# Weight loads of the second pass on GpSimd's DMA queue, pool-branch stores on SyncE's

## The chip, the core and the metric

The kernel runs on one core of a Trainium2 chip. The metric is the device time of one execution in microseconds (us). The engines are TensorE (PE in the rows), VectorE (DVE), ScalarE (ACT), GpSimd (POOL) and SyncE (SP); SP does nothing but issue transfers. Each issuing engine goes through its instructions in order: an instruction that waits for a semaphore holds up everything behind it on that engine, transfers included.

## What is computed

One hybrid encoder layer on x of 1024 x 2048 in float32, from the reference:

```python
h = rmsnorm(x, pre_g) * (1.0 + scale[:, None]) + shift[:, None]   # shift, scale, gate from silu(c) @ w_ada
q, k, v, gate_a, u, gate_p = jnp.split(h @ w_in, SPLIT_POINTS, axis=-1)      # w_in: 2048 x 4608
y_a = windowed_gqa(q, k, v, rel_table, sink) * jax.nn.silu(gate_a)           # 8 heads, window 128
y_p = multiscale_pool(u, w_pool_grp, pool_scale) * jax.nn.silu(gate_p)       # windows 2, 4, 8, 16
g_a, g_p = jnp.split(jax.nn.sigmoid(h @ w_merge + b_merge), 2, axis=-1)      # w_merge: 2048 x 4096
merged = g_a * (y_a @ w_br_attn) + g_p * (y_p @ w_br_pool)                   # branches: 1024 x 2048 each
o = merged @ w_out
return x + gate[:, None] * rmsnorm(o, post_g)
```

The pooling subtracts each token from the mean of a window around it, multiplies per group with a 256 x 256 matrix, and scales.

## The kernel before

Every float32 product is made of three fast ones: each operand is split into a high part (`hi`, ScalarE rounds it) and a low rest (`lo`, VectorE subtracts), and hi x hi, hi x lo and lo x hi are summed in PSUM. On top of that the large products use a scheme of Strassen's kind: 7 block products in place of 8, named B11, T3, T2, B21, T4, T1, B22 after the moving operand (`strassen`, line 183; `product`, line 203). One call of `strassen` is a *pair*: 256 columns of weights against half of the contraction (1024 rows). A product is 12 matmuls of 128 x 512, a pair 84. The results go through three kinds of PSUM banks, X, V and Z.

The projection by `w_in` and `w_merge` has 34 pairs of columns. The contraction is done in two passes: the first writes partial sums to DRAM (`part_d`), the second (`next_pair`, line 885) reads them back (`part<-part_d`, four loads of 256 KB per pair, line 180), adds, and stores the result to `proj_d` (line 282). Beside the second pass' pairs run, as `side` steps, the attention (`step`, line 1000) and then the pooling (`pool_steps`, line 1101). Then come the two branch products, attention and pool, 8 pairs each (line 1165), and the product by `w_out`.

The weights of a pair come as two loads of 512 KB (`load_raws`, line 162; the loads are line 173), one for each half of the contraction rows: tiles `raw` of 128 partitions x 4 pieces x 256 columns, thus 512 pieces of 1 KB. Four buffers hold two pairs. `fetch_weights` (line 287) is called at step 1 of a pair, and loads the weights of a later pair into the buffers of an earlier one as soon as VectorE has read these for the last time. From `raw` VectorE forms sums of blocks (`raw<-raw,raw`, line 104 or 107; `ws<-raw`), and `prep` (line 197) splits them into `whi` and `wlo`, four buffers each.

Before the change all these loads are issued by SP, whose queue also carries the partial sums, the stores of results, the gates `g` and stores `ya_d<-g` of the attention, and the gates `gt` of the branches. GpSimd (`side_load`, `side_store`, line 111) carries in the stretch of the change only the pooling's transfers: `u` (line 1040), the gate `sil` (line 1044, two buffers) and the store of the finished tile `yp_d<-sil` (line 1099); the next `sil` load into a buffer waits until the store from it has landed. `u` has two buffers, set free by VectorE. The order in which instructions stand on each engine is laid down when the program is built, by a scheduler that estimates durations; so a change of a queue can also move rows on VectorE and ScalarE.

Of the kernel before, what the change touches and what calls it, by code (L numbers as in the profile page):

```python
# [20 lines left out]
P = 128  # L21
# [21 lines left out]
def encoder_layer(ctx: ExitStack, tc: tile.TileContext, x, c, table, w_ada, b_ada, pre_g,  # L43
# [21 lines left out]
    def pool(name, bufs=1, **kw):  # L65
        return tc.tile_pool(name=name, bufs=bufs, reuse_waits="tile", **kw)
# [10 lines left out]
    def uid(s):  # L77
        cnt[0] += 1
        return f"{s}_{cnt[0]}"

    def bank(tag, name="b"):
        return psum.tile([P, 512], F32, tag=tag, name=uid(name), bufs=1 if tag in SEEDED else 2)
# [8 lines left out]
    def split(hi, lo, src):  # L91
        last_hi[0] = nc.scalar.activation(hi, src, AF.Copy)  # L92
        last_split[0] = nc.vector.tensor_tensor(lo, src, f32(hi), ALU.subtract)  # L93
        return last_split[0]
# [8 lines left out]
    def add(o, a, b, eng=None):  # L103
        (eng or nc.vector).tensor_tensor(o, a, b, ALU.add)  # L104
# [2 lines left out]
        (eng or nc.vector).tensor_tensor(o, a, b, ALU.subtract)  # L107

    load = nc.sync.dma_start
    store = nc.sync.dma_start  # L110
    side_load = side_store = nc.gpsimd.dma_start

# [21 lines left out]
    yp_d = dram.tile([NH * P, S], F32, name="yp_d")  # L134
# [23 lines left out]
    def ktile(kh, j):  # L158

        return 2 * j + kh  # L160

    def load_raws(w, n0, row0, js):

        nj = len(js)
        r0 = row0 + ktile(0, js[0]) * P
        rows = w[r0:r0 + 2 * nj * P, n0:n0 + 256].rearrange("(j k p) n -> k p j n", k=2, p=P)
        if nj == 2:
            r = wp.tile([P, 2, 2, 256], F32, tag="raw", name=uid("raw"), bufs=4)
            halves = [r[:, 0], r[:, 1]]
        else:  # L170
            halves = [wp.tile([P, 4, 256], F32, tag="raw", name=uid("raw"), bufs=4) for _ in range(2)]
        for kh in range(2):
            load(halves[kh], rows[kh])
        return [[h[:, :, nt * P:(nt + 1) * P] for h in halves] for nt in range(2)]

    def load_parts(ev, part):
# [110 lines left out]
    def fetch_weights():  # L287
        if wanted_w:
            fetched.append(load_raws(*wanted_w.popleft(), range(4)))
# [40 lines left out]
    rows = ev.tile([P, 512], F32, tag="ev", name="rows")[0:104, 0:P]  # L330
# [187 lines left out]
    def all_of(steps):  # L518
        for s_ in steps:
            s_()  # L520

    fetch_rows_of_x(0)
    fetch_rows_of_x(1)
    raws = [load_raws(*weight_of(ORDER[0]), 0, (0, 1))]
    ada = [ada_slots(0, load)]
    first_w = [slot("wf") for _ in range(3)]
# [39 lines left out]
    ada.append(ada_slots(1, load))  # L566
    claim((1,))
    raws += [load_raws(*weight_of(ORDER[i]), 0, (0, 1)) for i in (1, 2)]
    mark = const.tile([P, 1], F32, name="mark")
    come = ada[1][KT - 3][:, 0, 0:1]  # L570
# [120 lines left out]
    i = RAMP  # L691
# [111 lines left out]
    halves = deque()  # L803
# [75 lines left out]
    assert not side  # L879
    all_of(before)  # L880
    op = op2
    pidx = [0]
    side = deque()

    def next_pair(every=(0, 1, 3, 4, 6), then=None):
        n = ORDER[pidx[0]]
        w, n0 = weight_of(n)
        run(strassen(w, n0, HALF * P, range(4), op, to_dram(block(proj_d, n)),
                     block(part_d, n)), side, every, None, then)
        pidx[0] += 1  # L890
# [140 lines left out]
    with pool("pool") as pp:  # L1031
        pooled, sil = {}, {}

        us, sg, wg = {}, {}, {}

        def fetch_u(i):
            us[i] = pp.tile([P, S + 2 * PAD], F32, tag="u", name=f"u{i}", bufs=2)
            nc.gpsimd.memset(us[i][:, 0:PAD], 0.0)
            nc.gpsimd.memset(us[i][:, S + PAD:S + 2 * PAD], 0.0)
            side_load(us[i][:, PAD:PAD + S], proj_d[COL_U + i * P:COL_U + (i + 1) * P, :])  # L1040

        def fetch_sg(i):
            sg[i] = pp.tile([P, S], F32, tag="sil", name=f"sil{i}", bufs=2)
            side_load(sg[i], proj_d[COL_GP + i * P:COL_GP + (i + 1) * P, :])

        def fetch_wg(g):
            wg[g] = pp.tile([P, 2, 256], F32, tag="wg", name=f"wg{g}")
            load(wg[g], w_pg[g].rearrange("(k p) n -> p k n", p=P))

        def split_wg(g):  # L1050
            gh = pp.tile([P, 2, 256], F32R, tag="wgh", name=f"wgh{g}")
            gl = pp.tile([P, 2, 256], F32R, tag="wgl", name=f"wgl{g}")
            split(gh, gl, wg[g])
            wg[g] = gh, gl

        def window(i, w):

            cur, n = us[i], 1
            lo_, hi_ = 0, S + 2 * PAD
            while n < w:  # L1060
                if n == 4:
                    yield
                nxt = pp.tile([P, S + 2 * PAD], F32, tag="win", name=f"win{i}_{n}", bufs=2)
                d0, d1 = (1, 0) if n == 1 else (n // 2, n // 2)
                lo_, hi_ = lo_ + d0, hi_ - d1
                add(nxt[:, lo_:hi_], cur[:, lo_ - d0:hi_ - d0], cur[:, lo_ + d1:hi_ + d1])
                cur, n = nxt, 2 * n
            if w <= 4:
                yield
            win = cur[:, PAD:PAD + S]  # L1070
            for e in list(range(w // 2)) + list(range(S - w // 2 + 1, S)):
                n_e = min(S, e + w // 2) - max(0, e - w // 2)
                nc.vector.tensor_scalar(win[:, e:e + 1], win[:, e:e + 1], float(w) / n_e, None,
                                        op0=ALU.mult)
            yield
            nc.vector.scalar_tensor_tensor(win, win, 1.0 / w, us.pop(i)[:, PAD:PAD + S],
                                           op0=ALU.mult, op1=ALU.subtract)
            hi = pp.tile([P, S], F32R, tag="phi", name=f"phi{i}", bufs=2)
            lo = pp.tile([P, S], F32R, tag="plo", name=f"plo{i}", bufs=2)
            split(hi, lo, win)  # L1080
            pooled[i] = (hi, lo)
            yield

        def mix(g, j):
            i = 2 * g + j
            gh, gl = wg[g]
            t = sg.pop(i)
            wn = slice(j * P, (j + 1) * P)
            for s in range(2):
                sl = slice(s * 512, (s + 1) * 512)  # L1090
                ps = bank("at")
                for k in range(2):
                    hi, lo = pooled[2 * g + k]
                    nc.tensor.matmul(ps, gh[:, k, wn], hi[:, sl], start=k == 0, stop=False)
                    nc.tensor.matmul(ps, gh[:, k, wn], lo[:, sl], start=False, stop=False)
                    nc.tensor.matmul(ps, gl[:, k, wn], hi[:, sl], start=False, stop=k == 1)
                nc.vector.scalar_tensor_tensor(t[:, sl], ps, cols[:, 96 + i:97 + i], t[:, sl],
                                               op0=ALU.mult, op1=ALU.mult)
            side_store(yp_d[i * P:(i + 1) * P, :], t)

        def pool_steps(g, w):
            i = 2 * g
            first, second = window(i, w), window(i + 1, w)

            def silu(i):
                nc.scalar.activation(sg[i], sg[i], AF.Silu)

            return [lambda: (next(first), fetch_wg(g), fetch_u(i + 1)),
                    lambda: next(first),
                    lambda: (next(first), fetch_sg(i)),  # L1110
                    lambda: (next(second), split_wg(g)),
                    lambda: (next(second), fetch_sg(i + 1)),
                    lambda: (next(second), fetch_u(i + 2) if g < 3 else None),
                    lambda: (silu(i), silu(i + 1), mix(g, 0)),
                    lambda: mix(g, 1)]

        for g, w in enumerate(POOLS):
            side.extend(pool_steps(g, w))
        fetch_u(0)
        while side:  # L1120
            next_pair((1, 2, 4, 5))
        while side:
            next_pair((2, 5))
# [41 lines left out]
    for b, w in enumerate((w_ba, w_bp)):  # L1165
# [4 lines left out]
        else:  # L1170
# [6 lines left out]
            for _ in range(2):  # L1177
                t = mr.tile([P, 2, 512], F32, tag="raw2", name=uid("mt"), bufs=2)
# [424 lines left out]
```

## Time and profile before

| | us |
|---|---|
| median of 3 runs (lowest to highest) | 2133.7 (2130.52 to 2135.07) |
| the profiled execution | 2130.04 |
| its span, first to last instruction | 2128.0 |
| TensorE busy in the span | 2078.3 (98%) |
| VectorE busy | 1502.8 (71%) |
| ScalarE busy | 1082.4 (51%) |
| GpSimd busy | 195.6 (9%) |
| transfers of SP's queue (q1) | 345.58 MB |
| transfers of GpSimd's queue (q0) | 100.85 MB |

A share of busy time is an average over the whole span; what a stage can lose or gain is read from that stage's rows. The granted clock of TensorE is 1.00 of full speed in practically all of the span. The stages by time: the first pass to about 740 us, four plain pairs of the second pass to about 808, attention to about 1170, pooling to about 1362, plain pairs to about 1500, the branches to about 1830, then the product by `w_out`.

### The profile page before, as it was taken

To read this page: it belongs to the slowest core of one execution; us is meant where nothing else is said; L and a number is where in the kernel's file an instruction comes from. 1 tells how busy PE (TensorE), PEld (TensorE's weight loads), DVE (VectorE), ACT (ScalarE), POOL (GpSimd) and SP (SyncE) were. 2 spreads that over 40 slices of the span, in tenths; PEclk is the share of its full clock that TensorE was granted. 3 is DMA by queue.
4 is the path that set the end of the run, shared out by engine and by line. 5 is a ranking of instruction groups with operands and counts; after the bars stand their busy time and mean duration, and the time that the engine had idled before them with its cause. 6 is when DMAs were issued, how large, how long until landed. Compare 5 with 4: busy or idle time off the path is not lost.

```text
span 2128.0 us, 29020 instructions
## 1 busy us (share of the span) xinstructions
PE 2078.3 (98%) x9628; PEld 1709.8 (80%) x9628; DVE 1502.8 (71%) x2701; ACT 1082.4 (51%) x2005; POOL 195.6 (9%) x424
## 2 busy tenths in 40 slices
PE   5999999999999999999999999999999999999997
PEld 3688788888888888888888878788788887788886
DVE  6788577775456867777686678757857977655568
ACT  6664434443554635777676334234645645545343
POOL 1402132221022100000000000000000000000012
PEclk9999999999999999999999999999999999999999
DMA  9778688885566555555445666565665646877258
GB/s 343 279 232 308 227 279 294 285 294 172 170 214 226 191 183 188 165 165 193 159 163 158 213 217 216 190 214 174 202 208 167 205 139 203 271 245 235 96 177 306
DMA packets 268334, 455.62 MB, mean 214 GB/s; under 512 B 23538, under 2 KB 119930, under 8 KB 268184
## 3 DMA queue, kind: packets, MB, share of 16 engines
q1 hardware_dynamic: 234016, 345.58, 49.8%
q0 software_dynamic: 30256, 100.85, 14.1%
q10 hardware_dynamic: 3912, 7.34, 1.1%
q8 instruction: 76, 1.25, 0.2%
q14 instruction: 74, 0.61, 0.1%
HBM read 321.53 MB, written 134.24 MB: 214 GB/s over the span
## 4 chain that ended last, share of the span: by engine, by line
PE 85%; DMA 7%; DVE 5%; issue 2%; ACT 1%; SPq 0%; DVEq 0%; POOL 0%; ACTq 0%; POOLq 0%
PE Z L207 29%; PE V L207 20%; PE X L207 19%; PE OUT L1292 11%; DMA ada<-in_w_ada_dram 1%; DVE wlo L93 1%; DMA xt<-in_x_dram 1%; PE PT L980 1%; DVE po L1504 1%; DMA sil<-proj_d 1%; DMA m_d<-pv 1%; DMA proj_d<-p 1%; DMA lm<-m_d 1%; DMA pv<-mp_d 0%; PE SCORE L958 0%
## 5 line engine op out<-in xcount | busy, mean ns | idle before, releaser
L92 ACT ACTIVATE whi<-raw 128x512 fp32r<-128x512 f32 (+1 forms) x537 | 320.4, 601 | 456.5 <-PE Z L207 245.8
L93 DVE TENSOR_TENSOR wlo<-raw,whi 128x512 fp32r<-128x512 f32 (+1 forms) x537 | 347.8, 652 | 140.2 <-PE Z L207 78.1
L92 ACT ACTIVATE whi<-wr 128x512 fp32r<-128x512 f32 x112 | 69.6, 627 | 103.3 <-PE OUT L1292 95.4
L93 DVE TENSOR_TENSOR wlo<-wr,whi 128x512 fp32r<-128x512 f32 x112 | 75.8, 687 | 64.5 <-ACT whi L92 64.5
L104 DVE TENSOR_TENSOR u<-V,u 128x512 f32<-128x512 f32 x90 | 62.0, 689 | 73.5 <-PE V L207 70.0
L92 ACT ACTIVATE whi<-ws 128x512 fp32r<-128x512 f32 (+1 forms) x90 | 54.1, 601 | 109.2 <-PE V L207 107.8
L104 DVE TENSOR_TENSOR raw<-raw,raw 128x512 f32<-128x512 f32 x78 | 53.8, 689 | 59.3 <-DMA raw<-in_w_merge_dram 37.7
L207 PE MATMUL Z<-B22h,whi 128*128 128x512 f32 x334 | 92.0, 393 | 3.7 <-ACT u L256 2.4
L207 PE MATMUL V<-T3h,whi 128*128 128x512 f32 x334 | 91.6, 393 | 1.8 <-ACT whi L92 1.8
L207 PE MATMUL Z<-T1h,whi 128*128 128x512 f32 x334 | 91.0, 390 | 2.0 <-ACT u L218 1.5
L207 PE MATMUL X<-B11h,whi 128*128 128x512 f32 x334 | 91.7, 392 | 0.0
L207 PE MATMUL V<-T4h,whi 128*128 128x512 f32 x334 | 91.3, 392 | 0.0
L207 PE MATMUL Z<-T2h,whi 128*128 128x512 f32 x334 | 90.7, 391 | 0.4 <-ACT Z L233 0.4
L207 PE MATMUL X<-B21h,whi 128*128 128x512 f32 x334 | 90.8, 391 | 0.0
L207 PE MATMUL V<-T4l,whi 128*128 128x512 f32 x334 | 90.7, 390 | 0.0
L207 PE MATMUL Z<-B22l,whi 128*128 128x512 f32 x334 | 90.5, 390 | 0.0
L207 PE MATMUL V<-T3h,wlo 128*128 128x512 f32 x334 | 90.5, 390 | 0.0
L207 PE MATMUL V<-T3l,whi 128*128 128x512 f32 x334 | 90.5, 390 | 0.0
L207 PE MATMUL X<-B11l,whi 128*128 128x512 f32 x334 | 90.5, 390 | 0.0
L207 PE MATMUL X<-B21l,whi 128*128 128x512 f32 x334 | 90.4, 390 | 0.0
L207 PE MATMUL X<-B11h,wlo 128*128 128x512 f32 x334 | 90.4, 390 | 0.0
L207 PE MATMUL Z<-T1l,whi 128*128 128x512 f32 x334 | 90.4, 389 | 0.0
(418 smaller groups left out, 5108.9 us busy)
## 6 DMA issues: line engine op xcount, KB each, us to landing
part<-part_d SPq DMA_DIRECT2D x136, 256.0 KB, 4.1
raw<-in_w_merge_dram SPq DMA_DIRECT2D x64, 512.0 KB, 5.4
raw<-in_w_in_dram SPq DMA_DIRECT2D x60, 512.0 KB, 4.8
ada<-in_w_ada_dram POOLq DMA_DIRECT2D x96, 256.0 KB, 6.4
proj_d<-part SPq DMA_DIRECT2D x68, 256.0 KB, 2.2
gada<-in_w_ada_dram POOLq DMA_DIRECT2D x32, 512.0 KB, 5.8
gt<-proj_d SPq DMA_DIRECT2D x64, 256.0 KB, 3.2
wr<-ws_d SPq DMA_DIRECT2D x32, 512.0 KB, 4.9
```

The lines of the kernel that those rows point to most:

```text
L92: last_hi[0] = nc.scalar.activation(hi, src, AF.Copy)
L93: last_split[0] = nc.vector.tensor_tensor(lo, src, f32(hi), ALU.subtract)
L104: (eng or nc.vector).tensor_tensor(o, a, b, ALU.add)
L207: last_mm[0] = nc.tensor.matmul(ps, w_[:, i], op[mov][j][m_], start=fresh and i == 0 and n == 0, stop=i == nj - 1 and n == 2, skip_group_c ...
L980: nc.tensor.transpose(pt[:, i * P:(i + 1) * P], p[:, i * P:(i + 1) * P], ident)
L1292: nc.tensor.matmul(banks[t], m_[:, ts_], w_, start=fresh and j == 0 and n == 0, stop=j == KS - 1 and n == 2, skip_group_check=True)
L1504: last_lo[0] = nc.vector.scalar_tensor_tensor(o_, o_, s_[:, 2:3], rows_x[si][n], op0=ALU.mult, op1=ALU.add)
```

## The change

`load_raws` issues its loads through a cell, `raw_load[0]`. The cell holds SP's queue at first and is set to GpSimd's where the second pass begins, and stays so for the branches. The store of the pooling's finished tile goes from GpSimd's queue to SP's.

```diff
     load = nc.sync.dma_start
+    raw_load = [load]
     store = nc.sync.dma_start
     side_load = side_store = nc.gpsimd.dma_start
...
         for kh in range(2):
-            load(halves[kh], rows[kh])
+            raw_load[0](halves[kh], rows[kh])
...
     all_of(before)
     op = op2
+    raw_load[0] = side_load
     pidx = [0]
...
                 nc.vector.scalar_tensor_tensor(t[:, sl], ps, cols[:, 96 + i:97 + i], t[:, sl],
                                                op0=ALU.mult, op1=ALU.mult)
-            side_store(yp_d[i * P:(i + 1) * P, :], t)
+            store(yp_d[i * P:(i + 1) * P, :], t)
```

TensorE's order is the same before and after. GpSimd's order at the end of attention, where the pooling's first loads stand; before:

```order
L772 DMA ws_d_102<-xt_6564 128x512
L1038 MEMSET u_11549 128x8
L1039 MEMSET u_11549 128x8
L1040 DMA u_11549<-proj_d 128x1024
L1038 MEMSET u_11613 128x8
L1039 MEMSET u_11613 128x8
L1040 DMA u_11613<-proj_d 128x1024
L1044 DMA sil_11677<-proj_d 128x1024
L1044 DMA sil_11780<-proj_d 128x1024
```

The same place after the change (`raw_11585` and `raw_11586` are the two halves of one pair's weights):

```order
L174 DMA raw_11419<-in_w_merge_dram 128x4x256
L174 DMA raw_11585<-in_w_merge_dram 128x4x256
L1040 MEMSET u_11549 128x8
L1041 MEMSET u_11549 128x8
L1042 DMA u_11549<-proj_d 128x1024
L1040 MEMSET u_11613 128x8
L1041 MEMSET u_11613 128x8
L1042 DMA u_11613<-proj_d 128x1024
L1046 DMA sil_11677<-proj_d 128x1024
L174 DMA raw_11586<-in_w_merge_dram 128x4x256
L1046 DMA sil_11780<-proj_d 128x1024
```

The first two `u` loads, which stood behind nothing of this stage, now stand behind the weight half `raw_11585`, and the pair's other half behind both `u` loads and a gate.

SP's order where the first finished tiles of the pooling are stored; before (GpSimd stores `sil_11677` and `sil_11780` there):

```order
L282 DMA proj_d<-part_11559 128x512
L173 DMA raw_11951<-in_w_merge_dram 128x4x256
L282 DMA proj_d<-part_11727 128x512
L173 DMA raw_11952<-in_w_merge_dram 128x4x256
L282 DMA proj_d<-u_2394_11823 128x512
L180 DMA part_11919<-part_d 128x512
```

After:

```order
L283 DMA proj_d<-part_11559 128x512
L283 DMA proj_d<-part_11727 128x512
L1101 DMA yp_d<-sil_11677 128x1024
L283 DMA proj_d<-u_2394_11823 128x512
L1101 DMA yp_d<-sil_11780 128x1024
L181 DMA part_11919<-part_d 128x512
```

The two weight halves are gone from SP, and the two stores stand ahead of the next pair's partial sums.

ScalarE's order in the attention, at the Silu of one of its gates (`g_8296`); before:

```order
L92 ACTIVATE whi_8424<-raw_8070 128x512
L256 ACTIVATE u_1667_8274<-Z_8025 128x512
L92 ACTIVATE pp_8220<-PT_8278 128x3x128
L944 ACT_TABLE_LOAD
L944 ACTIVATE g_8296<-g_8296 128x512
```

After:

```order
L92 ACTIVATE whi_8424<-raw_8070 128x512
L946 ACT_TABLE_LOAD
L946 ACTIVATE g_8296<-g_8296 128x512
L257 ACTIVATE u_1667_8274<-Z_8025 128x512
L92 ACTIVATE pp_8220<-PT_8278 128x3x128
```

The Silu and its table load moved ahead of a copy of TensorE's result and of a split of attention weights. The same happens at one more gate, `g_11108`; the other 14 stand as before.

## Rows read from the trace of the kernel before

**Rows 1.** The page, part 1: busy us (share of the span) xinstructions of an engine.

```profile
PE 2078.3 (98%) x9628; PEld 1709.8 (80%) x9628; DVE 1502.8 (71%) x2701; ACT 1082.4 (51%) x2005; POOL 195.6 (9%) x424
```

**Rows 2.** Busy time by stage: stretch, its length, busy us (xinstructions) of each engine.

```profile
808.00:1170.00 362.00, 358.66 (x1846) 306.31 (x1845) 263.55 (x649) 251.68 (x531) 1.36 (x6) 1.00 0.53 170
1170.00:1362.00 192.00, 188.75 (x833) 155.42 (x832) 149.97 (x259) 69.40 (x107) 12.59 (x34) 1.00 0.65 207
1362.00:1500.00 138.00, 138.00 (x610) 114.12 (x609) 93.37 (x148) 52.74 (x88) 0.00 (x0) 1.00 0.62 197
1500.00:1830.00 330.00, 326.42 (x1433) 267.96 (x1432) 252.91 (x403) 186.04 (x320) 0.00 (x0) 1.00 0.59 192
```

**Rows 3.** Timeline of a plain pair: start, us, engine, line, out<-in [idle before <-releaser].

```profile
1414.95 0.68 DVE L93 TENSOR_TENSOR wlo<-raw,whi 128x512 fp32r<-128x512 f32 x1
...
1415.97 0.39 SPq L173 DMA_DIRECT2D raw<-in_w_merge_dram  x1
...
1419.85 0.69 DVE L93 TENSOR_TENSOR wlo<-raw,whi 128x512 fp32r<-128x512 f32 x1 [0.77 <-PE Z L207]
...
1421.06 0.69 DVE L104 TENSOR_TENSOR raw<-raw,raw 128x512 f32<-128x512 f32 x1
...
1429.55 1.07 PE L207 MATMUL Z<-T2h,wlo 128*128 128x512 f32 x4
```

**Rows 4.** GpSimd's load issues of two lines: duration ns min/median/max, first and last start.

```profile
L412 POOL DMA_DIRECT2D ada<-in_w_ada_dram x32: 722/722/771, 51.9 to 78.8; - x32
...
L451 POOL DMA_DIRECT2D ada<-in_w_ada_dram x64: 536/536/567, 179.6 to 336.7; - x64
```

**Rows 5.** DMA issues: out<-in, queue, xcount, KB each, median us to landing.

```profile
raw<-in_w_branch_attn_dram SPq DMA_DIRECT2D x16, 512.0 KB, 4.8
...
u<-proj_d POOLq DMA_DIRECT2D x8, 512.0 KB, 4.8
```

**Rows 6.** Busy time in the first pass; columns as in rows 2.

```profile
150.00:500.00 350.00, 348.72 (x1550) 287.63 (x1549) 260.07 (x376) 147.19 (x248) 89.50 (x168) 1.00 0.81 276
```

**Rows 7.** Timelines where attention ends and pooling begins.

```profile
1156.82 0.54 POOL L1040 DMA_DIRECT2D u<-proj_d  x1 [0.36 <-issue]
...
1157.39 0.38 SPq L173 DMA_DIRECT2D raw<-in_w_merge_dram  x1
...
1164.39 0.69 DVE L104 TENSOR_TENSOR raw<-raw,raw 128x512 f32<-128x512 f32 x1 [3.88 <-DMA raw<-in_w_merge_dram]
...
1166.84 0.41 PE L980 MATMUL PT<-ident,p 128*128 128x128 f32 x2 [1.58 <-DVE g L995]
...
1174.84 0.38 SPq L173 DMA_DIRECT2D raw<-in_w_merge_dram  x1
...
1186.00 1.23 DVE L104 TENSOR_TENSOR win<-u 128x1039 f32<-128x1039 f32 x1
```

**Rows 8.** Timelines at the first finished tile of the pooling.

```profile
1221.15 0.54 POOL L1099 DMA_DIRECT2D yp_d<-sil  x1 [13.02 <-issue]
...
1226.35 0.53 POOL L1044 DMA_DIRECT2D sil<-proj_d  x1 [4.66 <-DVE sil L1097]
...
1233.16 1.06 ACT L1106 ACTIVATE sil<-sil 128x1024 f32<-128x1024 f32 x1 [5.47 <-DMA sil<-proj_d]
...
1234.76 1.19 PE L207 MATMUL Z<-B22h,whi 128*128 128x512 f32 x4 [1.43 <-ACT u L256]
```

**Rows 9.** A gate of the attention that holds up ScalarE, and TensorE's wait behind it.

```profile
1054.02 1.28 ACT L944 ACT_TABLE_LOAD   x1 [2.82 <-DMA g<-proj_d]
...
1066.50 1.21 PE L207 MATMUL V<-T3h,whi 128*128 128x512 f32 x4 [1.76 <-ACT whi L92]
```

**Rows 10.** SP's queue at another gate: weight load, stores of the attention, gates.

```profile
873.05 0.38 SPq L173 DMA_DIRECT2D raw<-in_w_in_dram  x1
873.52 0.99 SPq L998 DMA_DIRECT2D ya_d<-g  x2
...
878.52 1.28 SPq L943 DMA_DIRECT2D g<-proj_d  x2
```

## The prediction

> **What bounds the kernel now.** I read the page first: TensorE is busy for 2078.3 us of a span of 2128.0, 98% [rows 1]. Whatever the change does to queues can show in the time only where TensorE waits, or where a new wait is made to reach it. So the second view is the busy time by stage over the part of the span in which nearly all moved transfers lie. Its rows give TensorE's idle time by subtraction: attention 362.00 - 358.66 = 3.34 us, pooling 192.00 - 188.75 = 3.25, the plain pairs behind it 0, the two branches 330.00 - 326.42 = 3.58 [rows 2]. Together 10.2 us, 0.48% of the span: more than that the change can't give back. It can cost more.
>
> Third view, the timeline of one plain pair, to see how much room a weight load has. VectorE's last read of the old tile starts at 1414.95 and takes 0.68 us; SP issues the load into that tile at 1415.97. The new tile is first wanted by the addition at 1421.06, which follows its predecessor without a wait: the load lands just in time. But what VectorE makes there is far ahead of TensorE: the low half of a weight made at 1419.85 (done at 1420.54) is read by TensorE at 1429.55, 9.0 us later [rows 3]. A late weight load first stalls VectorE, and only after some 9 us TensorE.
>
> **The change part by part.** In the order of instructions TensorE's rows are word for word the same, SP loses 98 loads of 512 KB and gains 8 stores, GpSimd the reverse. Nothing is computed or moved more or less.
>
> *SP loses 98 issues.* At 0.39 us each [rows 3] that is 38 us of SP, but SP is not what TensorE waits for: the row behind a weight load on SP is mostly a store that waits for VectorE itself. Value 0; the bounds are those of the sum below.
>
> *GpSimd gains 98 issues.* Its load issue takes 536 ns for 128 rows of 2 KB and 722 ns for 256 pieces of 1 KB [rows 4]. A weight load has 512 pieces of 1 KB; going on with 186 ns for each further 128 pieces gives an estimate of 536 + 3 x 186 = 1094 ns, 0.7 us more than SP. From issue to landing 512 KB took 4.8 us on either queue [rows 5], so I let a weight land 0 to 0.7 us later than now and take 0.7. The load can't leave earlier: its buffer comes free by VectorE's read, as seen above. VectorE then stalls up to 0.7 us per pair at the addition; the 9.0 us of [rows 3] hide this. Value 0, bounds 0 and, if the cover is gone in the pooling stage, +5.7 us (the rival below).
>
> VectorE doesn't seem to hold up GpSimd's issues: where GpSimd issues most, with VectorE busy for 260.07 of 350 us [rows 6], its 64 issues from one line lie between 536 and 567 ns [rows 4]. The Trainium skill (SBUF — State Buffer, section "SBUF: two separate sides") speaks against this change: a transfer issued by GpSimd has its descriptors written by GpSimd itself, which is locked out while VectorE runs one of its two-port modes. By that rule 98 loads could each be held back for a VectorE instruction. No issue here shows it, so the sum leaves it at 0 and it is a rival.
>
> *GpSimd's row order at the end of attention.* This is where I expect a gain. Now GpSimd is empty and sends the first two u tiles (512 KB each) early, the second at 1156.82. SP's second weight half leaves at 1157.39 and lands only when VectorE's addition starts, at 1164.39: 7.0 us instead of 4.8, after 3.88 us of idling. Behind that addition on VectorE stands the gating of the attention output, and TensorE waits 1.58 us for it, at 1166.84 [rows 7]. In the new order both u tiles stand behind a weight half that can't leave before 1174.8 (SP sent it at 1174.84, when its buffer was free). They are then no longer in the way at 1157; a landing after 4.8 + 0.7 us would start the addition at 1162.9, 1.5 us sooner, and the wait of 1.58 us goes, up to 0.1. Value -1.6, bounds 0 and -1.6. What is late next: the first u tile leaves at about 1176.3 (weight issue 1.1 us, memsets 0.4) and lands about 1181.1; its first reader runs at 1186.00 [rows 7]. 4.9 us are left, in a stretch with another 1 MB in it.
>
> *The pool branch's stores go to SP.* Now GpSimd stores a finished tile at 1221.15, then stands until that store has landed, for the next gate's load needs the buffer: load at 1226.35, Silu on ScalarE at 1233.16 after 5.47 us of idling, and behind the Silu the copy for which TensorE waits 1.43 us at 1234.76 [rows 8]. In the new order SP issues that store with nothing but a store of an earlier block ahead, and GpSimd's queue no longer holds the second store (1 us later than it could be) behind the first load. The store itself must still land before the load. From 5.2 us (1221.15 to 1226.35) down to a typical landing of 4.8 less half a microsecond of issue, Silu starts 0.5 to 1 us sooner; the next Silu of the group, whose store stood behind the load, by 1 to 2. I take the whole -1.4 since the same store also leaves a queue on which its landing was waited for; bounds 0 and -1.4. Its price on SP: the four partial-sum loads behind the second store wait some 3 us for VectorE, and they are wanted a product later; 0.
>
> *Gates of attention.* Two of the 16 Silus of the attention gates move up on ScalarE, by two rows, ahead of a copy of TensorE's result. A Silu that waits for its gate holds ScalarE: 2.82 us at 1054.02, and TensorE then lost 1.76 us at 1066.50 [rows 9]. Twice that is the upper bound, +3.5. Against it: in both of these places the store whose landing the gate's load awaits stood directly behind a weight load on SP (873.05, 873.52), and the gate's load left only at 878.52 [rows 10]; with the weight load elsewhere the store lands sooner. Value 0, bounds -1.8 (the wait at 1066.50 goes too) and +3.5.
>
> By the Trainium skill (DMA: Bandwidth & Descriptors, section "Issuing engines are not separate DMA queues") transfers from all issuers end up on the same 16 engines, and spreading them saves only issue time: by that the gains just named would be near 0, and the forecast no change at all.
>
> Sum: -1.6 - 1.4 + 0 = -3.0 us against the profiled execution's 2130.04 (span 2128.0 and 2.0 around it). That run lies 3.7 us under the median of three, 2133.7; on the median the sum gives 2130.7, 0.14% faster. This kernel's runs lie within about 0.2% of each other (2130.52 to 2135.07), so 4.3 us is what can be told from no change.
>
> **Rivals.**
> - *Nothing comes through: 2133.7.* At each of the two places something else ends last: the weight half lands late at 1162 for the other transfers there, and the Silu waits for its load as before. For it: the store-to-load chain of [rows 8] keeps both its steps. Against it: only 1 to 2 us are needed in each.
> - *All queue waits go: 2127.0.* Stores and gates on SP no longer share a queue with weights, and the waits at 1066.50 (1.76) and one like it among the 3.25 us of the pooling stage and the 3.58 of the branches (some 2 us) go as well: -3.0 - 1.8 - 2.0 = -6.8. For it: [rows 9, 10]. Against it: the branches' waits are behind gate loads that wait for VectorE.
> - *Slower, late weights in the pooling stage: 2139.4.* There GpSimd's queue carries weights, u tiles and gates in one order, and VectorE is busy 149.97 of 192 us [rows 2]. If the 0.7 us of each later landing reaches TensorE in the 8 pairs of this stage, it costs 8 x 0.71 = 5.7 us and covers the gains. It decides from the point at which VectorE's lag passes the 9.0 us of [rows 3], or where the first u tile lands after 1186.00. Against it: 42 us of idling of VectorE in the stage, 5 per pair.
> - *GpSimd's issues are held back by VectorE.* A VectorE instruction of 0.7 us per load, 98 x 0.68 = 67 us if all reached TensorE, 2200; with the cover of 9 us in all plain pairs only the 8 pairs of pooling would show it, which is the case above once more, 2139. Against it: [rows 4, 6].
>
> **How the numbers follow.** The forecast (its own range 2128.5 to 2132.7) has 0.47, nothing comes through 0.25, all waits go 0.14, late weights 0.11, held-back issues 0.03. Faster by over 0.2% takes the third case and a quarter of the forecast's lower flank, 0.26; slower by over 0.2% the last two less a little and a part of the second's scatter, 0.14; the rest, 0.60, is within 0.2%. The range goes from 2126 (all waits go, and 1 us of scatter) to 2139 (late weights).
>
> **What would show it.** Right: the first u tile's load on GpSimd at about 1176 and the addition at 1164.39 some 1.5 us sooner, with no wait of TensorE for the attention's gating; Silu waits in the pooling stage shorter than 5.47 us; GpSimd's weight issues near 1.1 us; TensorE's idle time from 740 to 1830 near 7 us instead of 10.2. Wrong: weight landings beyond 6 us and a line "TensorE waits for ScalarE's or VectorE's weight halves" of several microseconds; VectorE waiting for u at 1186; ScalarE idling before the two Silus moved up and TensorE behind it.

## The result: slower, and where the profile after shows it

Six runs of the changed kernel have a median of 2147.67 us (2144.92 to 2150.15), six of the kernel before 2132.3 us; the ratio is 1.0072 [1.0061, 1.0083], 15.4 us slower. The forecast was 2130.7 with a range of 2126 to 2139. The two profiled executions have spans of 2147.2 and 2128.0 us, 19.2 apart.

Busy time by stage in the kernel after; columns are stretch, length, busy us (and instructions) of TensorE, its weight loads, VectorE, ScalarE, GpSimd, then granted clock, DMA share, GB/s:

```profile
808.00:1170.00 362.00, 357.46 (x1835) 304.59 (x1834) 262.86 (x647) 249.81 (x528) 21.07 (x29) 1.00 0.51 167
1170.00:1380.00 210.00, 201.66 (x873) 164.86 (x872) 153.93 (x269) 73.59 (x114) 23.27 (x50) 0.98 0.64 205
1380.00:1500.00 120.00, 120.00 (x531) 99.34 (x531) 76.14 (x121) 41.68 (x69) 8.99 (x12) 1.00 0.64 197
1500.00:1840.00 340.00, 333.33 (x1453) 272.77 (x1452) 260.84 (x417) 185.88 (x321) 22.46 (x30) 0.99 0.58 184
```

Length less TensorE's busy time gives its idle time: attention 4.54 us (3.34 before), pooling 8.34 (3.25), plain pairs 0 (0), branches 6.67 (3.58). In these wider stretches the kernel before idles exactly as in [rows 2]. Together 19.55 against 10.17: 9.4 us of the 19.2. Another 2.9 arose ahead of all that the change touches (attention's first score product starts at 816.5 instead of 813.6): in the first pass of this execution the clock fell while TensorE was busy all along, to a mean of 0.77 over 15 us, 3.4 us lost; the kernel before shows 1.00 in that stretch. Most of the rest is the clock, too. Four stretches of the kernel after, same columns, the first of them in the first pass:

```profile
510.00:525.00 15.00, 15.00 (x71) 12.66 (x70) 4.74 (x10) 3.68 (x6) 0.51 (x1) 0.77 0.12 41
1330.00:1340.00 10.00, 7.86 (x28) 6.09 (x27) 7.32 (x23) 6.14 (x9) 0.00 (x0) 0.83 0.33 116
1370.00:1380.00 10.00, 10.00 (x38) 8.05 (x37) 5.62 (x10) 2.29 (x4) 0.00 (x0) 0.83 0.81 264
1810.00:1820.00 10.00, 7.89 (x28) 5.99 (x27) 7.58 (x12) 7.08 (x13) 0.00 (x0) 0.83 0.49 161
```

A mean granted clock of 0.83 over 10 us is 1.7 us lost (3.4 us at 1.2 instead of 2.4 GHz), and in the last three stretches it stands right behind TensorE's three longest waits here: 2.14, 2.26 and 2.11 us. In the kernel before no wait of these stages exceeds 1.76 us [rows 9] and the clock stays at 1.00. Three times 1.7 is 5.1 us: 9.4 + 2.9 + 5.1 = 17.4 of 19.2.

The borders of the stretches cut the two executions at different rows. The same matmul taken from both, which is possible because TensorE's rows stand in the same order, closes the account: it starts 2.9 us later at the start of attention, 5.2 at its end, 14.2 at the end of pooling and of the plain pairs, and 19.3 at the end of the branches. So attention costs 2.3 us in this execution, pooling 9.0, the plain pairs 0 and the branches 5.1.

What TensorE waits for from 808 to 1840, as groups (line, operation, shapes, xcount | busy us, mean ns | idle us ahead of them and what ended it):

```profile
L208 PE MATMUL Z<-B22h,whi 128*128 128x512 f32 x188 | 52.7, 402 | 6.8 <-ACT u L257 6.8
L208 PE MATMUL Z<-T2h,whi 128*128 128x512 f32 x184 | 49.6, 391 | 4.0 <-ACT Z L234 4.0
L992 PE MATMUL PV<-pp,v 128*128 128x256 f32 x88 | 25.2, 286 | 1.8 <-ACT pp L92 1.8
L1096 PE MATMUL b<-phi,wgh 128*128 128x512 f32 x32 | 13.3, 415 | 2.3 <-DVE sil L1099 2.3
```

The first three are copies or halves made by ScalarE that stand behind a Silu or Sigmoid whose gate has not landed; the last is a PSUM bank that VectorE frees late. (Line numbers are 1 or 2 above those of the kernel before.) Three places show the pattern.

*The row order.* Which row stands where on VectorE and ScalarE is not written in the kernel; it is laid out when the program is built, and the new queues changed it: about 105 of VectorE's 2701 rows and 37 of ScalarE's 2005 stand elsewhere, TensorE's nowhere. Some 85 of them lie in attention, 8 in pooling, 9 in the plain pairs and 37 in the branches. VectorE in one plain pair, before and after:

```
before
1821 L93 TENSOR_TENSOR wlo_13474<-raw_13275,whi_13473 128x512
1822 L104 TENSOR_TENSOR p_2628_13297<-p_2628_13297,u_2640_13391 128x512
1823 L104 TENSOR_TENSOR raw_13431<-raw_13431,raw_13432 128x4x128
after
1821 L104 TENSOR_TENSOR raw_13431<-raw_13431,raw_13432 128x4x128
1822 L93 TENSOR_TENSOR wlo_13474<-raw_13275,whi_13473 128x512
1823 L104 TENSOR_TENSOR p_2628_13297<-p_2628_13297,u_2640_13391 128x512
```

The addition that needs a freshly loaded weight has moved ahead of the low half that TensorE reads and of a finished result. The timeline of such a pair in the kernel after, the answer to [rows 3]:

```profile
1429.15 0.68 DVE L93 TENSOR_TENSOR wlo<-raw,whi 128x512 fp32r<-128x512 f32 x1
...
1430.13 0.75 POOL L174 DMA_DIRECT2D raw<-in_w_merge_dram  x1 [4.69 <-DVE wlo L93]
...
1432.58 0.69 DVE L107 TENSOR_TENSOR ws<-raw 128x512 f32<-128x512 f32 x1
...
1435.80 0.69 DVE L104 TENSOR_TENSOR raw<-raw,raw 128x512 f32<-128x512 f32 x1 [2.52 <-DMA raw<-in_w_merge_dram]
```

From the freeing row to the addition it is 6.65 us, before 6.11: 0.54 us more, within the 0 to 0.7 of the forecast. But VectorE now stalls 2.52 us, with two rows behind the stall that did not need the load. On ScalarE the same happened to gates; a branch in the kernel after, where the Sigmoid now precedes the copy Z that TensorE waits for:

```profile
1712.18 0.73 ACT L1194 ACTIVATE gt<-gt,cols 128x512 f32<-128x512 f32 x1 [1.85 <-DMA gt<-proj_d]
1712.81 0.58 ACT L234 ACTIVATE Z<-X 128x512 f32<-128x512 f32 x1
...
1713.44 1.20 PE L208 MATMUL Z<-T2h,whi 128*128 128x512 f32 x4 [0.56 <-ACT Z L234]
```

The branches' longest wait, 2.11 us at 1812.64, is not of this kind: the Sigmoid ahead of that copy has its old place, and only its gate lands later (ScalarE idles 3.54 us for it, 2.07 before).

One of the attention's two Silus that moved up (the prediction's "up to +3.5") costs TensorE 0.43 us, the other 0.85 and 0.43. At a third gate, whose Silu did not move, TensorE loses 0.91 and 0.41. The first:

```profile
883.87 0.63 ACT L946 ACTIVATE g<-g 128x512 f32<-128x512 f32 x1 [0.88 <-DMA g<-proj_d]
884.41 0.58 ACT L257 ACTIVATE u<-Z 128x512 f32<-128x512 f32 x1
884.89 0.48 ACT L92 ACTIVATE pp<-PT 128x384 fp32r<-128x384 f32 x1
...
886.24 0.39 PE L993 MATMUL PV<-pp,v 128*128 128x256 f32 x1 [0.43 <-DVE pp L93]
```

*Where attention ends* (timeline of the kernel after, the answer to [rows 7]; this execution is 5.1 us behind here):

```profile
1168.18 0.69 DVE L104 TENSOR_TENSOR raw<-raw,raw 128x512 f32<-128x512 f32 x1 [0.71 <-DMA raw<-in_w_merge_dram]
...
1180.29 0.75 POOL L174 DMA_DIRECT2D raw<-in_w_merge_dram  x1 [15.93 <-DVE wlo L93]
...
1181.12 0.55 POOL L1042 DMA_DIRECT2D u<-proj_d  x1
...
1181.73 0.55 POOL L1042 DMA_DIRECT2D u<-proj_d  x1
1182.36 0.53 POOL L1046 DMA_DIRECT2D sil<-proj_d  x1
1185.73 0.76 POOL L174 DMA_DIRECT2D raw<-in_w_merge_dram  x1 [2.84 <-DVE wlo L93]
...
1189.53 1.24 DVE L104 TENSOR_TENSOR win<-u 128x1039 f32<-128x1039 f32 x1 [1.37 <-DMA u<-proj_d]
...
1195.05 0.69 DVE L104 TENSOR_TENSOR raw<-raw,raw 128x512 f32<-128x512 f32 x1 [3.61 <-DMA raw<-in_w_merge_dram]
```

The addition stalls 0.71 us instead of 3.88, and TensorE has no wait for the gated output: the forecast's first gain came. Its price came too. Five loads of 512 KB leave within 5.4 us, the first u tile needs 8.4 us to its reader instead of the 4.8 of [rows 5], and VectorE loses 1.37 and 3.61 us. Over these rows TensorE falls back by another 1.1 us (5.18 to 6.29).

*A pool tile* (timeline of the kernel after, the answer to [rows 8]): store, gate load, Silu, TensorE's wait.

```profile
1226.83 0.32 SPq L1101 DMA_DIRECT2D yp_d<-sil  x1
...
1233.03 0.55 POOL L1046 DMA_DIRECT2D sil<-proj_d  x1 [7.15 <-DVE sil L1099]
...
1239.86 1.06 ACT L1108 ACTIVATE sil<-sil 128x1024 f32<-128x1024 f32 x1 [5.88 <-DMA sil<-proj_d]
...
1241.46 1.20 PE L208 MATMUL Z<-B22h,whi 128*128 128x512 f32 x4 [1.84 <-ACT u L257]
```

Store to Silu is 13.0 us; before it was 12.0. At the stage's four pairs of gates TensorE waits 0.68, 1.84, 1.42 and 2.14 us for this copy (before: none, 1.43, 0.29 and none), and 2.26 us for a PSUM bank at the stage's end (1.52 before); that is the stage's 8.34 us. The 2.14 us, and VectorE's row behind the 2.26:

```profile
1331.11 1.06 ACT L1108 ACTIVATE sil<-sil 128x1024 f32<-128x1024 f32 x1 [6.17 <-DMA sil<-proj_d]
1332.07 0.58 ACT L257 ACTIVATE u<-Z 128x512 f32<-128x512 f32 x1
...
1332.70 2.07 PE L208 MATMUL Z<-B22h,whi 128*128 128x512 f32 x4 [2.14 <-ACT u L257]
...
1360.19 0.69 DVE L104 TENSOR_TENSOR p<-V,part 128x512 f32<-128x512 f32 x1 [4.44 <-DMA proj_d<-p]
```

The wait at the stage's end is not for a weight or a gate: VectorE idles 4.44 us (3.62 before) until a store on SyncE's queue has landed, and frees the bank after that. Every kernel below has this wait, from 1.6 to 2.6 us.

### The profile page after: what moved, and what is told of

It reads as the page before. It is cut to its first block, busy times and chain, and to the rows that moved or that the text cites. A ratio compares the mean times of both kernels' runs of the same rounds, so it can differ in the third digit from the quotient of the medians.

```text
span 2147.2 us, 29051 instructions
## 1 busy us (share of the span) xinstructions
PE 2087.5 (97%) x9628; PEld 1715.1 (80%) x9628; DVE 1501.2 (70%) x2701; ACT 1081.2 (50%) x2005; POOL 265.3 (12%) x514
## 4 chain that ended last, share of the span: by engine, by line
PE 79%; DMA 8%; issue 7%; DVE 5%; ACT 1%; POOL 0%; SPq 0%; DVEq 0%; ACTq 0%; POOLq 0%
PE Z L208 27%; PE X L208 18%; PE V L208 18%; PE OUT L1294 11%; DMA sil<-proj_d 1%; DMA xt<-in_x_dram 1%; DVE wlo L93 1%; DMA m_d<-pv 1%; DMA gt<-proj_d 1%; DMA ada<-in_w_ada_dram 1%; DVE po L1506 1%; PE GEMV L429 1%; PE PT L982 1%; DMA lm<-m_d 0%; DMA pv<-mp_d 0%
## 5 line engine op out<-in xcount | busy, mean ns | idle before, releaser
L1194 ACT ACTIVATE gt<-gt,cols 128x512 f32<-128x512 f32 x64 | 46.2, 722 | 91.8 <-DMA gt<-proj_d 83.1
L208 PE MATMUL Z<-T2h,wlo 128*128 128x512 f32 x334 | 91.1, 392 | 0.0
L208 PE MATMUL Z<-T2l,whi 128*128 128x512 f32 x334 | 90.8, 391 | 0.0
```

The source lines that it names most:

```text
L208: last_mm[0] = nc.tensor.matmul(ps, w_[:, i], op[mov][j][m_], start=fresh and i == 0 and n == 0, stop=i == nj - 1 and n == 2, skip_group_c ...
L1194: nc.scalar.activation(gt, gt, AF.Sigmoid, bias=cols[:, col:col + 1])
```

## The experiments

All twelve were timed against the kernel before. Idle time of TensorE is from the stage view of each kernel's profiled execution, one for each kernel; that of e12 took 5.7 us longer than its kernel's median.

| kernel | ratio to before, 95% interval | idle us: attention, pooling, branches |
|---|---|---|
| before | 1 | 3.34, 3.25, 3.58 |
| after | 1.0072 [1.0061, 1.0083] | 4.54, 8.34, 6.67 |
| e1_stores | 0.9998 [0.9990, 1.0007] | 3.20, 2.26, 3.43 |
| e2_weights | 1.0069 [1.0056, 1.0082] | 4.58, 7.12, 5.08 |
| e3_pool_sp | 1.0029 [1.0017, 1.0041] | 4.88, 3.89, 3.15 |
| e4_branch_sp | 1.0059 [1.0046, 1.0072] | 5.72, 8.32, 3.27 |
| e5_rows | 1.0042 [1.0027, 1.0058] | 2.90, 9.06, 2.33 |
| e6_rows_sp | 0.9999 [0.9988, 1.0009] | 2.95, 2.50, 3.00 |
| e8_first | 1.0057 [1.0041, 1.0072] | 3.67, 5.70, 6.35 |
| e9_att_only | 1.0012 [1.0001, 1.0024] | 4.96, 2.40, 2.69 |
| e10_rows_pool_sp | 1.0011 [0.9999, 1.0023] | 3.95, 2.03, 3.10 |
| e11_pool_only | 1.0025 [1.0016, 1.0033] | 1.37, 8.71, 2.03 |
| e12_rows_first | 1.0026 [1.0016, 1.0036] | 4.34, 8.31, 3.41 |
| e15_better | 0.9996 [0.9984, 1.0008] | 1.38, 3.97, 3.45 |

These idle times leave out what the clock costs. TensorE's order is the same in all kernels, so the delay of the same matmul against the kernel before takes both in. By attention, pooling and branches it grows by 2.3, 9.0 and 5.1 us in the kernel after; 4.1, 0.7 and -0.3 in e3; 5.1, 7.5 and -0.5 in e4; 0.0, 9.7 and -1.5 in e5; -2.3, 7.7 and -2.1 in e11; in the plain pairs by 0 in every kernel. These too are single executions.

### Stores or weights: e1_stores, e2_weights

e1 is the kernel before with one line changed; e2 is the changed kernel with that line put back.

```
e1  -            side_store(yp_d[i * P:(i + 1) * P, :], t)
    +            store(yp_d[i * P:(i + 1) * P, :], t)
e2  -            store(yp_d[i * P:(i + 1) * P, :], t)
    +            side_store(yp_d[i * P:(i + 1) * P, :], t)
```

> The kernel before, with the pool branch's eight stores alone on SyncE's queue; weights stay on SyncE. Theory S (the moved stores are the loss in the pooling stage: stores land later on SP, so the gate load on GpSimd, the Silu and TensorE's copy come later, three waits of 1.4 to 2.1 us and the clock behind them): the pooling stage grows by 7 to 8 us, time 2139 to 2141, Silu loads 6.2 us behind the first store of a group as in the changed kernel. Theory W (the moved weights are the loss): time 2130.5 to 2132.5, Silu loads at most 5.2 us behind the store, no TensorE wait above 1.5 us in the pooling stage.

> The changed kernel with the eight stores back on GpSimd's queue: the weight loads alone are moved. Theory W: nearly the changed kernel's time, 2145 to 2149. Theory S: the pooling stage's 7 to 8 us are gone, 2139 to 2141. If both take part: above 2149, since the second store of a group now also stands behind weight loads on GpSimd.

Measured 2129.46 and 2145.22 us. Theory S falls: the stores alone cost nothing, the weights alone (with the row order that comes with them, which e2 shares with the changed kernel) nearly all. e1 leaves the rows of TensorE, VectorE and ScalarE word for word as they were, so it also tests the forecast's second gain. Its timeline at the first finished tile:

```profile
1222.20 0.32 SPq L1099 DMA_DIRECT2D yp_d<-sil  x1
...
1226.00 0.53 POOL L1044 DMA_DIRECT2D sil<-proj_d  x1 [18.55 <-DMA yp_d<-sil]
...
1229.54 1.06 ACT L1106 ACTIVATE sil<-sil 128x1024 f32<-128x1024 f32 x1 [0.19 <-DMA sil<-proj_d]
```

Store to Silu takes 7.3 us instead of 12.0, ScalarE waits 0.19 instead of 5.47, and TensorE's 1.43 us for the copy are gone. A longer wait at the stage's end (2.26 for 1.52) takes part of it back: 1.0 us less idle in pooling, too little for the times to show.

### Which stage: e3_pool_sp, e4_branch_sp, e9_att_only, e11_pool_only

The changed kernel, with the loader switched at stage borders (e3: SyncE in pooling; e4: SyncE in the branches; e9: GpSimd only up to the end of attention; e11: GpSimd in pooling only).

```
e3  +        raw_load[0] = load          # behind fetch_u(0)
    +        raw_load[0] = side_load     # behind pooling's last pair
e4  +    raw_load[0] = load              # ahead of the two branches
e9  +        raw_load[0] = load          # behind fetch_u(0), for all that follows
e11 -    raw_load[0] = side_load         # ahead of the second pass
    +        raw_load[0] = side_load     # behind fetch_u(0)
    +        raw_load[0] = load          # behind pooling's last pair
```

> The changed kernel, but in the pooling stage (from the first u tile to the last mix) weights are loaded through SyncE's queue; stores stay on SyncE. Theory W: the pooling stage's 8 us go, 2139 to 2141, and the first u tile leaves near 1157 again instead of 1181. Theory S: 2146 to 2148, waits of 1.4 to 2.1 us stay in the pooling stage.

> The changed kernel, but the weights of the two branches are loaded through SyncE's queue. If the weights on GpSimd are what delays the branches' gate loads, Sigmoids and copies (idle TensorE 6.7 us instead of 3.6 between 1500 and 1830, and the clock behind it), the branches' 5 us go: 2142 to 2144. If that part is a matter of one execution or comes from the stages ahead: 2147 to 2148.

> The changed kernel with weights on GpSimd from the second pass to the end of attention only; pooling, the plain pairs and the branches load theirs through SyncE. If attention costs nothing, as the sum of the two earlier runs suggests: 2129.5 to 2132.5, with the gain forecast for the end of attention in it if that is real (then the lower end). If attention costs the 2 us that its longer idle time shows: 2132.5 to 2135.

> Weights on GpSimd in the pooling stage alone, stores on SyncE, everything else as before; the order differs from the kernel before in some eight rows at the stage's start. If the pooling loss stands by itself: 2139 to 2142, with Silu waits near 6 us and clock dips behind the longest waits of TensorE. If it needs VectorE's lag from the attention stage or the moved rows elsewhere: 2133 to 2136.

Measured 2135.86, 2141.91, 2134.03 and 2136.11 us. Against the 15.3 us of the changed kernel (0.0072 of 2131), pooling's weights back on SyncE save 9.2, the branches' 2.8 (intervals overlap; the idle time falls from 6.67 to 3.27), and attention alone costs 2.6. Moving the loads back moves rows back, too: e3 has pooling's 8 moved rows in their old places, e4 the branches' 37, e9 all but attention's 85. These three show the queue and the order together.

Weights on GpSimd in pooling alone cost 5.3, less than the 9.2 that their removal saves. That does not make pooling's own loss smaller: e11 idles there as long as the changed kernel (8.71 against 8.34 us) and falls back by 7.7 us, and gets part of it back in attention and the branches, where it idles 2.0 and 1.6 us less than the kernel before. DMA issues from 1170 to 1380 (queue, xcount, KB each, median us to landing) in the kernel before, after, and e3:

```profile
raw<-in_w_merge_dram SPq DMA_DIRECT2D x20, 512.0 KB, 5.0
...
sil<-proj_d POOLq DMA_DIRECT2D x8, 512.0 KB, 4.9
```

```profile
raw<-in_w_merge_dram POOLq DMA_DIRECT2D x18, 512.0 KB, 6.1
...
sil<-proj_d POOLq DMA_DIRECT2D x8, 512.0 KB, 6.3
```

```profile
raw<-in_w_merge_dram SPq DMA_DIRECT2D x16, 512.0 KB, 4.6
...
sil<-proj_d POOLq DMA_DIRECT2D x8, 512.0 KB, 4.8
```

In pooling a weight half lands 1.1 to 1.5 us later on GpSimd's queue, and so does the gate that the Silu needs. e11 also isolates the forecast's first gain, since its attention stage has the old rows and the old queue, and only the u tiles leave late (1176.86). Its stage row:

```profile
808.00:1170.00 362.00, 360.63 (x1855) 308.36 (x1854) 265.59 (x652) 252.15 (x531) 0.00 (x0) 1.00 0.51 170
```

TensorE idles 1.37 us there instead of 3.34: the wait of 1.58 for the gated output is gone.

### Row order or late landing: e5_rows, e6_rows_sp

e5 is the changed kernel with the order of before forced on VectorE and ScalarE (some 14 rows differ); e6 the kernel before with the new order in the plain pairs and branches. In the plain pairs e6 has the changed kernel's order; in the branches 31 of its rows stand in still other places, and attention's 85 rows are left as before.

```
+    for first, second in rows_to_keep:          # rows that changed place, in the wanted order
+        tc.add_manual_dep(second, first.name, NoSync)
```

> The changed kernel with the order of instructions on ScalarE and VectorE held to that of the kernel before (all but some 14 rows), weights on GpSimd. Theory R (the loss in the branches, and part of the pooling stage's, is the order: additions and gates placed ahead of the rows that make or free what TensorE reads, so that one late transfer holds them): the branches' 6 us go, 2139 to 2142, and the pooling stage keeps its 7 to 8 us of waits. Theory L (late landing of the weights alone): 2145 to 2149.

> The kernel before, weights on SyncE, with ScalarE's and VectorE's rows of the plain pairs and the branches put in the order of the changed kernel. Theory R: slower by 3 to 6 us, 2134 to 2138, ScalarE's idle time ahead of the gates from 1500 to 1830 above 75 us. Theory L: no change, 2130 to 2133: the order costs nothing while the weights land as before.

Measured 2139.72 and 2130.21 us: each theory loses one. With the old order the changed kernel gains 6.4 us (0.0072 to 0.0042): attention's and the branches' idle time falls below that of the kernel before, pooling's stays. But the new order with weights on SyncE, as far as e6 has it, costs nothing, though VectorE stalls. VectorE's additions in the plain pairs, in e6 and in the kernel after (the first row counts both kinds, the second only the one that waits; the kernel before has 3.0 us):

```profile
L1620 DVE TENSOR_TENSOR raw<-raw,raw 128x512 f32<-128x512 f32 x12 | 8.3, 691 | 7.9 <-DMA raw<-in_w_merge_dram 7.0 <-DMA raw<-in_w_branch_attn_dram 0.7
```

```profile
L104 DVE TENSOR_TENSOR raw<-raw,raw 128x512 f32<-128x512 f32 x6 | 4.2, 693 | 12.1 <-DMA raw<-in_w_merge_dram 10.5 <-DMA raw<-in_w_branch_attn_dram 1.6
```

So 3.0 becomes 7.9 by the order alone and 12.1 by order and queue together. In the plain pairs neither reaches TensorE. In the branches the loss is gone with the old order (e5: idle 2.33), with the old order and SyncE (e4: 3.27), and with e6's order and SyncE (3.00): it seems to take both, though no run has exactly the new order there with weights on SyncE. For attention that test was not made. In pooling the order is not the cause: with the old order e5 falls back by as much there (9.7 us) as the changed kernel (9.0).

### The parts of pooling: e8_first, e10_rows_pool_sp, e12_rows_first

e8 is the changed kernel with only pooling's first pair on SyncE; e12 the same with the old order; e10 has the old order and all of pooling on SyncE.

```
e8, e12 +        raw_load[0] = load
        +        next_pair((1, 2, 4, 5))
        +        raw_load[0] = side_load
         while side:
             next_pair((1, 2, 4, 5))
```

> The changed kernel, but the weights of the first pair of the pooling stage alone go through SyncE's queue, so that the first u tiles aren't behind them on GpSimd (load near 1163 instead of 1181). Theory U (the first u tile's lateness shifts windows, mixes, stores and gates of the whole stage): pooling waits fall to 3 or 4 us, 2137 to 2141. Theory L: only the first wait (0.7 us) goes, the later ones stay, 2145 to 2147.

> The changed kernel with VectorE's order of the kernel before (and ScalarE's but for some four rows) and the pooling stage's weights on SyncE; weights on GpSimd in attention, the plain pairs and the branches. If order and pooling are the whole loss: 2127 to 2131, at or just under the kernel before, with TensorE's idle time at most 3 us in each of attention, pooling and branches, although VectorE's waits for weights stay longer than before. If late weights cost TensorE by themselves outside pooling too: 2134 or more.

> As the first of these three, but in the pooling stage only the first pair's weights are on SyncE. It splits the pooling loss with the order held: the first u tiles behind weights on GpSimd (theory U) against the later pairs' weights (theory L). U: 2130 to 2133. L: 2137 to 2140. About half each, as the changed kernel's run with this edit had it: 2134 to 2137.

Measured 2142.89, 2132.88 and 2136.21 us. The first pair is worth 3.2 us with the new order (after to e8) and 3.4 with the old (e5 to e12), the later pairs 3.2 (e12 to e10). Each of these is a difference of two ratios that is itself uncertain by 3 to 4 us, and e8 also puts pooling's 8 rows back: only the 6.6 us of both together (e5 to e10) are clear of noise, the even split is not shown. The times lie between the two theories. What is left in e10, 2.3 us, can't be told from 0 by its interval; attention's idle time, 3.95, and the branches', 3.10, are above the 3 that the expectation allowed. e12's profiled execution was its slowest (2141.89), so its idle times are above its median's.

### A version drawn from it: e15_better

Weights on SyncE, the first two u tiles on SyncE too, the pool tile stored by halves, order of before but for three rows:

```
-            side_load(us[i][:, PAD:PAD + S], proj_d...)
+            (load if i < 2 else side_load)(us[i][:, PAD:PAD + S], proj_d...)
-            side_store(yp_d[i * P:(i + 1) * P, :], t)
+                store(yp_d[i * P:(i + 1) * P, sl], t[:, sl])
```

> A version drawn from the runs: the kernel before with weights on SyncE, each pool store on SyncE in two halves of 256 KB (the first leaves when the first half of the tile is done), the first two u tiles on SyncE behind the weight half that they used to overtake, and ScalarE's and VectorE's order held to that of the kernel before but for three rows. If the wait for the gated output at the end of attention (1.5 us) and half of the pooling stage's 2.3 to 3.3 us go: 2127 to 2129.5. If the u tiles on SyncE come too late for the first windows, or the gains are under what the runs can tell: 2130 to 2132.

Measured 2130.32 against 2129.49 us, no difference. Attention's idle time falls by 2.0 us as in e11, but the u tiles leave at 1173.42 and 1174.99 and pooling's idle time rises by 0.7, with the clock falling once behind a wait of 1.96 us. None of the twelve kernels beats the kernel before by more than the runs can tell.

## Why the prediction was wrong, step by step

- *A weight lands 0 to 0.7 us later, hidden by the 9.0 us of [rows 3], value 0.* The step that failed: a mechanism, not a size. The stores alone cost nothing and the weights alone 14.7 us (e1, e2). In the plain pairs, where the 9.0 us were read, the cover held: 0.54 us later, and TensorE loses 0. In pooling it didn't: the halves land 1.1 us later, the gates on the same queue 1.4, and a Silu that waits for its gate holds a copy that TensorE reads 0.6 us later (1332.07 to 1332.70), not 9.0. TensorE idles 8.34 us instead of 3.25 there, and the clock falls twice behind these waits. Pooling's weights back on SyncE save 9.2 us (e3), with the old order held 6.6 (e5 to e10).
- *The rival "late weights in the pooling stage", 8 x 0.71 = 5.7 us.* It named the stage and had a chance of 0.11. That its number is near the measured 5.3 (e11) and 6.6 is in part luck: the loss is not 0.7 us in each of 8 pairs, but four waits behind Silus, a longer one at the end, and the clock.
- *"TensorE's rows are word for word the same", two Silus on ScalarE, value 0.* The second step that failed, a term left out. The statement is true of TensorE; of ScalarE's order it prices two Silus and of VectorE's nothing, while some 140 rows had moved on the two. Holding them back gains 6.4 us (e5), where pooling's weights are already on SyncE 3.8, barely clear of noise (e3 to e10); the delays put it in attention and the branches. With weights on SyncE the order cost nothing as far as e6 has it, so this term seems to exist only together with the first. It was missing from the sum and from the rivals.
- *The clock.* No term of the sum: behind three waits it cost 1.7 us each, 5.1 of 19.2.
- *GpSimd's issues, estimate 1094 ns.* They take 748 ns; the estimate was too high, and nothing hung on it.
- *End of attention, -1.6.* Came, in the changed kernel as in e11 (idle 3.34 to 1.37). But "4.9 us are left" for the first u tile was mis-sized: the landing of 4.8 us was taken from a median of the whole span, and it took 8.4 to the reader with four other loads of 512 KB around it. The kernel before already shows slow landings at this place, for the gates that leave at 1175.19 and 1175.77 (loads from 1174 to 1177, median us to landing):

```profile
sil<-proj_d POOLq DMA_DIRECT2D x2, 512.0 KB, 9.2
```

The first pair's 3.2 us (after to e8) are more than the gain; how much of them is the u tile's is not separated.

- *Stores to SyncE, -1.4.* The wait of 1.43 went in e1; 1.0 us of idle time remained saved. In the changed kernel it drowned in the later landings (1.84 us at the same place).
- *Issues held back by VectorE.* Did not happen. GpSimd's weight issues in the kernel after (ns min/median/max, first and last start), two of four groups:

```profile
L174 POOL DMA_DIRECT2D raw<-in_w_in_dram x34: 748/748/773, 726.4 to 1114.3; - x34
L174 POOL DMA_DIRECT2D raw<-in_w_merge_dram x32: 748/748/763, 1129.6 to 1468.2; - x32
```

All 98 lie between 748 and 773 ns. By the Trainium skill (SBUF — State Buffer, section "SBUF: two separate sides") GpSimd can't write descriptors while VectorE runs in a two-port mode; no issue here shows such a stall. A delay that comes behind the issue would not show in these rows.

The sum as measured: order 6.4, first pair of pooling 3.4, later pairs 3.2, rest 2.3, together the 15.3 us (after to e5 to e12 to e10 to before; each step is a difference of two ratios and uncertain by 3 to 4 us). The shares depend on the path: by after to e3 to e10 to before they are pooling 9.2, order elsewhere 3.8, rest 2.3.

By the Trainium skill (DMA: Bandwidth & Descriptors, section "Issuing engines are not separate DMA queues") transfers of all issuers interleave on the same engines, and spreading them over issuers saves only issue time. No view here shows which engine moved which load, but the prediction's reading of it, no change at all, did not come true: in pooling the moved loads land 1.1 us later beside SyncE's traffic than within it. Why they do is open: GpSimd's longer issue (0.75 against 0.38 us), the two queues side by side and a delay behind the issue are not separated.

## What to carry to other kernels

Moving a transfer to another queue can move rows on engines that issue none, here some 140: compare the order on every engine, and price each row that now stands ahead of what the busiest engine reads. Read the cover of a late load in every stage that it touches. Here it cost nothing in the plain pairs, where only its own consumer waited, and 9 us in pooling, where the queue also carried gates and ScalarE's copies stood behind them. A landing time read as a median over the span doesn't hold where several loads leave together: look up what loads take at that place (9.2 us for the two gates here, not 4.8).

## What the hardware showed that was not expected

The same 512 KB load takes 0.38 us to issue on SyncE and 0.75 on GpSimd, and in pooling lands after 4.6 (e3) to 5.0 us (before) on the one queue and 5.7 (e4) to 6.1 (after) on the other.

The granted clock fell to 1.2 GHz for a short while, a mean of 0.83 over 10 us, behind waits of TensorE of 2.11, 2.14 and 2.26 us (kernel after), 2.57 (e3) and 2.58 (e11), but also behind one of 1.78 (e8). It stayed at 1.00 behind waits of 2.26 (e1), 2.27 (e5) and 2.47 us (e12). So the length of the wait alone doesn't tell; where the clock fell, a wait near 2 us cost nearly twice its length. In the first pass of the kernel after it fell with no wait at all (0.77 over 15 us in which TensorE was busy for 15.00), which alone moves one execution by 3.4 us.
